# Attention in paired key tiles, and the conditioning's rows summed on VectorE with a short product on TensorE

## The chip, the cores and the metric

One core of a Trainium2 chip runs the whole kernel in one launch. The metric is the device time in microseconds (us). The engines that matter are TensorE (PE in the profile, PEld for its weight loads), VectorE (DVE), ScalarE (ACT), GpSimd (POOL) and SyncE (SP), whose queue issues most of the loads. Every engine works through its instructions in an order that is fixed when the kernel is built, and waits on semaphores for what others owe it.

## The reference, cut to what matters

The network is four layers on 256 rows (and, in the first layer, 256 rows of context) of width 1024, all in float32. The first two are "trunk" layers, the last two "hybrid" layers (a gated delta rule and a convolution branch). This is what the change touches:

```
def trunk_layer(x, ctx, c, c_ctx, p, ...):
    shift, scale, gate = split(silu(c) @ p['w_ada'] + p['b_ada'], 3)
    shift_c, scale_c, gate_c = split(silu(c_ctx) @ p['w_ada'] + p['b_ada'], 3)
    h  = x   * (1 + scale)   + shift          # context: hc, with the _c rows
    ... = split(h @ p['w_in'], pts)           # q, k, v, gates, decay inputs, ...
    y_attn = softmax(q k^T / 8) v * silu(a_g) # 8 heads of 64 on 2 key/value heads
    # gated linear attention (decay from (h @ w_a) @ a2 + ab), a spatial gating
    # unit, three branches merged, then
    x_new = layer_norm(ALPHA * x + gate * out, ...)
```

Layer 0 attends with 256 latent rows over 512 keys and with 256 context rows over 256 keys; layer 1 with the latent rows alone. `w_ada` is 1024 by 3072 for each layer: its product with the two vectors silu(c) and silu(c_ctx) gives shift, scale and gate, which this text calls the conditioning's rows. The hybrid layers need a small product of the same kind as the decay inputs (16 columns, called wab below).

## The kernel before

**Numbers.** A weight arrives as a 128x1024 piece of 512 KB through SP's queue into a ring of three buffers (`raw`, L232). `split` (L212) makes two fp32r halves of it, the high one by a cast on ScalarE (L214, `wh`) and the low one by a subtraction on VectorE (L215, `wl`). `mm3` (L220) multiplies with three fp32r matmuls: high by high, high by low, low by high. All of them go through one helper, so they carry the line L218; transposes carry L227.

**Order of the work.** A scheduler at build time sets one order per engine. It takes the program's order as priority, except where a piece is marked urgent, or is held `behind` another instruction. Layer 0 of the trunk starts with the conditioning of shift and scale for layer 0 (L417, in the first 43 us), then come the attention and the spatial gating unit together (about 49 to 252 us), the gated linear attention and the branches (to about 523 us) and the output norm. `PACES` (L170) says how many units of the branches are taken between the steps of the linear attention.

**The conditioning's rows.** What remains of them (gate of layer 0; shift, scale and gate of layer 1) is made by the generator `adaln` (L993) out of `ada_part` (L424). There are 4 parts of 8 pieces. For each piece the weight of 128x1024 is loaded into the same ring, and four plain f32 matmuls with a stationary of 128x32 (silu of the two vectors in its columns) and 256 moving columns each go side by side into four column tiles of the array (L433). Each f32 matmul has two records in the profile. The generator is drawn on between other steps of the layer (`fill`, L1004).

**Attention** (L628 to L770). For each tile of 128 rows and each pair of heads, the queries are transposed and split (`qh`, `ql`, 128x256, two buffers each), two score products per head follow (L218, `px<-kk,qh` and `px<-kk,ql`), then the maximum on VectorE (L748), the exponential on ScalarE (L749) and the norm on VectorE (L753). The probabilities are transposed for two key tiles at once into one bank (L227), split into `ph` (ScalarE) and `pl` (VectorE), and multiplied with the split values `vh` and `vl` by `mm3`: six matmuls of 256 columns for a tile, a key/value head and a key tile, taken over its two pairs. There are 24 such triples in layer 0 and 16 in layer 1, 40 in all.

**Small products.** The decay inputs (L773 to L797) and the wab product (start of `delta`, L1318) take `mm3` with a stationary of 32 and of 16 columns: three matmuls for each of 8 slices.

Of the kernel before, what the change touches and what calls it, by code (L numbers as in the profile page):

```python
# [17 lines left out]
P = 128  # L18
# [162 lines left out]
class Builder:  # L181
# [100 lines left out]

    def gemm_mv(self, keys, actT, tiles, evac):
# [31 lines left out]
    def build(self):  # L315
        nc, tc, io = self.nc, self.tc, self.io
        self.filler = iter(())
        with tc.tile_pool(name="const", bufs=1) as cp, \
# [23 lines left out]
            self.zero = cp.tile([P, 32], F32, name="zero")  # L342
            nc.vector.memset(self.zero, 0.0)
# [15 lines left out]
    def first_block(self):  # L359
        self.hTh = self.t(self.act, [P, KT, 512], F32R, tag="hTh")  # L360
        self.hTl = self.t(self.act, [P, KT, 512], F32R, tag="hTl")
        self.paT = self.t(self.act, [33, 512], tag="paT")
        self.nc.vector.memset(self.paT[32:33, :], 1.0)
# [7 lines left out]
    def start(self, sp):  # L371
# [30 lines left out]
        for name, to in (("mask", self.mask), ("maskc", self.maskc)):  # L402
            m = self.t(sp, list(to.shape), tag=name)
            nc.sync.dma_start(m, io[name])
            nc.gpsimd.tensor_copy(to, m)
# [18 lines left out]
    def ada_part(self, pool, l, part, out):  # L424

        nc = self.nc
        row = self.t(pool, [P, 256], tag="arow")
        nc.scalar.dma_start(row, self.io["bada"][l, part])
        ps = self.pa()
        for k in range(8):  # L430
            raw = self.raw(("ada", l, part, k))
            for q in range(4):
                self.nc.tensor.matmul(ps[32 * q:32 * q + 32, :256], self.sc[:, k, :], raw[:, 256 * q:256 * (q + 1)],  # L433
                                      start=k == 0, stop=k == 7, tile_position=(0, 32 * q))
            if k < 7:
                yield
        if part == 2:
            nc.vector.tensor_tensor(row, ps[:, :256], row, ALU.add)
            for v in ((0, 1) if l == 0 else (0,)):
                for q2 in range(2):  # L440
                    pt = self.psg()
                    for b in range(2):
                        r = 32 * (2 * q2 + b) + v
                        self.mm(pt[:, b * 256:(b + 1) * 256], self.ident[:, r:r + 1].to_broadcast([P, P]), row, True, True)

                    nc.scalar.activation(out[v][:, q2 * 512:(q2 + 1) * 512], pt, AF.Copy, scale=0.5)
        else:
            nc.vector.scalar_tensor_tensor(row, ps[:, :256], self.upper, row, ALU.add, ALU.add)
            pt = self.psg()
            for c in range(2):  # L450
                self.tr(pt[:, c * P:(c + 1) * P], row[:, c * P:(c + 1) * P])
            for a in range(2):
                src = pt[:, :256].rearrange("p (c a b v) -> p a b c v", c=2, a=2, b=2)[:, a, :, :, 0:2]
                dst = out[:, a, 4 * part:4 * part + 4, :].rearrange("p (b c) v -> p b c v", b=2)
                nc.vector.tensor_copy(dst, src)
        yield

    def trunk(self, l):
# [4 lines left out]
        with tc.tile_pool(name=f"m{l}", bufs=1) as mp:  # L463
            self.mp = mp
            if l == 0:
                self.yraw_a = self.big([P, 4, TN], tag="ya")
                self.yraw_g = self.big([P, 4, TN], tag="yg")
                self.m = [self.big([P, 4, TN], tag=f"m{i}") for i in range(2)]
# [6 lines left out]
            next(self.decay, None)  # L475
            with tc.tile_pool(name=f"sgu{l}", bufs=1) as sp:
                self.attention(l)
                self.sgu(l, sp)
            if l == 0:
                self.filler = self.adaln(mp)  # L480
            tgp = mp if l else tc.alloc_tile_pool(name="tg", bufs=1, side="right", reuse_waits="tile")
            units = self.units(l, tgp)
            pre0, rate0, mid, rate1 = PACES[l]
            for n, rate, hp in ((pre0, rate0, 0), (mid, rate1, 1)):
                for _ in range(int(n)):
                    next(units, None)
                due = 0.0
                for _ in self.gla(l, hp):
                    due += rate
                    while due >= 1:  # L490
                        due -= 1
                        next(units, None)
            for _ in units:
                pass
            self.fill(4)
            for _ in self.gate_y(l, G_G, self.yraw_g):
                pass
            with tc.tile_pool(name=f"late{l}", bufs=1, reuse_waits="tile") as lp:
# [5 lines left out]
                self.fill(32)  # L504
                if l:
                    self.out_ln(l)
                else:
                    tgp.release()
# [3 lines left out]
    def units(self, l, tgp):  # L512
# [4 lines left out]
        yield from self.gates(l, M_G, "tg", tgp)  # L517


    def sgu(self, l, sp):  # L520
# [36 lines left out]
        for g in range(4):  # L557
# [3 lines left out]
            mix = self.t(sp, [P, nt, P], tag="mix")  # L561
# [66 lines left out]
    def attention(self, l):  # L628
        nc, tc, io = self.nc, self.tc, self.io
        T0, TN = self.T0, self.TN  # L630
        with tc.tile_pool(name=f"att{l}", bufs=1, reuse_waits="tile") as ap:
# [59 lines left out]
            for i in range(4):  # L691
# [21 lines left out]
                vh[i] = self.t(ap, [P, 2, 64], F32R, tag=f"vh{i}")  # L713
                vl[i] = self.t(ap, [P, 2, 64], F32R, tag=f"vl{i}")
                self.split(vh[i], vl[i], kv[i][:, 128:256].rearrange("p (g d) -> p g d", g=2))
# [12 lines left out]
            for i in self.tiles:  # L728
                nk = 256 if i < 2 else 512
                for pr in range(4):  # L730
                    g = pr // 2
                    tp = self.ps()
                    if pr % 2 == 0:
                        du = self.t(ap, [P, 4, 2, 64], tag="du", bufs=2)
                        nc.scalar.copy(du, qkv[i][:, pr * P:(pr + 2) * P].rearrange("p (a b) -> p a b", a=4)[:, :, None, :].to_broadcast([P, 4, 2, 64]))
                    for a in range(2):
                        self.tr(tp[:, a * P:(a + 1) * P], du[:, pr % 2 * 2 + a].rearrange("p a b -> p (a b)"))
                    qh = self.t(ap, [P, 256], F32R, tag="qh", bufs=2)
                    ql = self.t(ap, [P, 256], F32R, tag="ql", bufs=2)
                    self.split(qh, ql, tp[:, :256])  # L740
                    mx = self.t(self.small, [P, 2], tag="mx")
                    sm = self.t(self.small, [P, 2], tag="sm")
                    pp = self.t(ap, [P, 2, nk], tag="pp", bufs=2)
                    for a in range(2):
                        s = self.ps()
# [1108 lines left out]
```

## Time and profile before

| | us |
|---|---|
| median of three runs | 1475.38 (1471.76 to 1478.45) |
| the profiled execution's own time | 1476.65 |
| its span | 1475.0 |
| TensorE busy in the span | 1406.7 (95%) |
| VectorE busy | 1024.1 (69%) |
| ScalarE busy | 846.9 (57%) |
| GpSimd busy | 70.2 (5%) |

All times below are of the profiled execution; its span leaves 1.65 us around it. The granted clock of TensorE was 0.99 of full speed over the span, so 2.4 GHz nearly throughout. "Busy" of TensorE is the union of matmul records, which overlap: from one start to the next is the better price of a matmul.

### The profile page before, as it was taken

How to read it: one execution, taken by the hardware profiler on the slowest of the kernel's cores; microseconds unless marked ns; L12 is line 12 of the kernel's file. 1: busy time of each engine (PE TensorE's matmuls, PEld its weight loads, DVE VectorE, ACT ScalarE, POOL GpSimd, SP SyncE). 2: the span in 40 equal slices, each digit the busy share in tenths (PEclk: the TensorE clock that was granted, in tenths of full speed). 3: DMA queues.
4: the chain of work that ended last, by engine and by line, in shares of the span. 5: the costliest groups of instructions: out<-in, count | busy, mean ns of one | idle time of the engine just before them, and what ended most of it. 6: DMA issues, size and time to landing. Idle time of an engine off the chain costs nothing.

```text
span 1475.0 us, 33026 instructions
## 1 busy us (share of the span) xinstructions
PE 1406.7 (95%) x13736; PEld 1233.2 (84%) x13736; DVE 1024.1 (69%) x2017; ACT 846.9 (57%) x1530; POOL 70.2 (5%) x228
## 2 busy tenths in 40 slices
PE   7999999999999999999999999879999999989998
PEld 4887778767876778998999999869889998979997
DVE  3576752874277248879847748877998776799885
ACT  2455644643374233555658576468695657967654
POOL 0000000110011000120000001011000000000000
PEclk9999999999999999999999999989999999999999
DMA  9321123234333346433324434614333553433362
GB/s 380 133 72 60 59 84 115 93 108 151 104 114 105 129 137 206 146 111 123 101 87 143 131 115 137 212 58 135 116 98 128 170 173 101 131 102 107 124 196 91
DMA packets 52901, 187.47 MB, mean 127 GB/s; under 512 B 6148, under 2 KB 7556, under 8 KB 52752
## 3 DMA queue, kind: packets, MB, share of 16 engines
q1 hardware_dynamic: 49248, 176.63, 36.3%
q0 software_dynamic: 2208, 7.35, 1.6%
q8 instruction: 108, 1.77, 0.5%
q10 hardware_dynamic: 1296, 1.39, 0.3%
q14 instruction: 41, 0.34, 0.1%
HBM read 184.29 MB, written 1.05 MB: 126 GB/s over the span
## 4 chain that ended last, share of the span: by engine, by line
PE 76%; DVE 10%; ACT 8%; issue 3%; DMA 2%; POOL 0%; SPq 0%; ACTq 0%; DVEq 0%; POOLq 0%
PE pg L218 57%; PE px L218 11%; PE px L227 3%; ACT wh L214 3%; DVE wl L215 2%; DMA raw<-in_W 2%; PE pa L433 1%; PE px L916 1%; DVE u L1721 1%; PE pa L218 1%; PE pa L417 1%; PE px L972 1%; PE px L1534 1%; PE px L950 1%; DMA araw<-in_W 0%
## 5 line engine op out<-in xcount | busy, mean ns | idle before, releaser
L215 DVE TENSOR_TENSOR wl<-raw,wh 128x1024 fp32r<-128x1024 f32 (+1 forms) x278 | 338.6, 1220 | 217.9 <-ACT wh L214 216.5
L218 PE MATMUL pg<-hTh,wh 128*128 128x256 f32 (+1 forms) x1440 | 460.2, 320 | 0.8 <-DVE mix L562 0.8
L214 ACT CAST wh<-raw 128x1024 fp32r<-128x1024 f32 (+1 forms) x278 | 289.3, 1043 | 284.0 <-PE pg L218 198.2
L218 PE MATMUL pg<-hTh,wl 128*128 128x256 f32 (+1 forms) x1440 | 450.1, 313 | 0.0
L218 PE MATMUL pg<-hTl,wh 128*128 128x256 f32 (+1 forms) x1440 | 449.9, 312 | 0.0
L218 PEld LDWEIGHTS pg<-hTh,wh 128*128 128x128 f32 x1440 | 271.5, 189 | 30.4 <-issue 12.5
L218 PEld LDWEIGHTS pg<-hTl,wh 128*128 128x128 f32 x1440 | 271.9, 189 | 15.9 <-issue 3.0
L218 PEld LDWEIGHTS pg<-hTh,wl 128*128 128x128 f32 x1440 | 271.1, 188 | 14.8 <-issue 0.4
L1721 DVE SCALAR_TENSOR_TENSOR u<-cpad,cols,u 128x256 f32<-128x256 f32 x240 | 104.6, 479 | 0.9
L218 PE MATMUL pg<-big,wh 128*128 128x512 f32 (+1 forms) x384 | 100.9, 345 | 4.2 <-DVE tg L620 1.4
L218 PE MATMUL pg<-wh,hTh 128*128 128x256 f32 x320 | 91.4, 286 | 0.6 <-ACT kd L817 0.6
L218 PE MATMUL pg<-wl,hTh 128*128 128x256 f32 x320 | 91.1, 285 | 0.0
L218 PE MATMUL pg<-wh,hTl 128*128 128x256 f32 x320 | 91.0, 285 | 0.0
L218 PEld LDWEIGHTS pg<-big,wh 128*128 128x128 f32 x384 | 65.9, 188 | 15.5 <-DVE big L215 2.1
L218 PE MATMUL pg<-wh,mh 128*128 128x256 f32 x272 | 77.1, 285 | 0.3 <-DVE y L1281 0.3
L218 PE MATMUL pg<-wl,mh 128*128 128x256 f32 x272 | 76.8, 283 | 0.3 <-DVE wl L215 0.3
L218 PE MATMUL pg<-wh,ml 128*128 128x256 f32 x272 | 76.8, 283 | 0.0
L218 PE MATMUL pg<-big,wl 128*128 128x512 f32 (+1 forms) x192 | 65.2, 341 | 0.0
L218 PEld LDWEIGHTS pg<-wh,hTh 128*128 128x128 f32 x320 | 61.2, 191 | 1.2 <-ACT kd L817 1.1
L218 PEld LDWEIGHTS pg<-wh,hTl 128*128 128x128 f32 x320 | 61.2, 191 | 0.1
L218 PEld LDWEIGHTS pg<-wl,hTh 128*128 128x128 f32 x320 | 61.1, 191 | 0.0
L218 PEld LDWEIGHTS pg<-wh,mh 128*128 128x128 f32 x272 | 51.9, 191 | 0.8 <-issue 0.4
(457 smaller groups left out, 2526.5 us busy)
## 6 DMA issues: line engine op xcount, KB each, us to landing
raw<-in_W SPq DMA_DIRECT2D x314, 512.0 KB, 3.5
araw<-in_W SPq DMA_DIRECT2D x16, 512.0 KB, 9.5
xT<-in_xT SPq DMA_DIRECT2D x4, 512.0 KB, 9.9
yg<-in_xtok POOLq DMA_DIRECT2D x2, 512.0 KB, 4.3
m<-in_xtok POOLq DMA_DIRECT2D x2, 512.0 KB, 6.1
nwrow<-in_nwrow POOLq DMA_DIRECT2D x2, 512.0 KB, 4.3
arow<-in_bada ACTq DMA_DIRECT2D x4, 128.0 KB, 2.8
wsT<-in_sguw POOLq DMA_DIRECT2D x2, 256.0 KB, 4.0
```

The source lines that it names most:

```text
L214: self.nc.scalar.copy(h, src)
L215: self.nc.vector.tensor_tensor(l, src, h.bitcast(F32), ALU.subtract)
L218: self.last_mm = self.nc.tensor.matmul(out, lhsT, rhs, start=start, stop=stop).ins
L227: self.nc.tensor.transpose(out, in_, self.ident[:k, :k])
L417: nc.tensor.matmul(ps[32 * g:32 * g + 32, :P], self.sc[:, k, :], raw[:, o:o + P], start=k == 0, stop=k == 7, tile_position=(0, 32 * g))
L433: self.nc.tensor.matmul(ps[32 * q:32 * q + 32, :256], self.sc[:, k, :], raw[:, 256 * q:256 * (q + 1)], start=k == 0, stop=k == 7, tile_pos ...
L916: nc.tensor.matmul(out[o, a, :], x[:, a, o], y[:, a, o], start=True, stop=True, tile_position=(0, 32 * b))
L950: nc.tensor.matmul(pa[ks, a, ts], e[ch, li, a, ks], qe[ch, li, a, ts], start=True, stop=True, tile_position=(64 * d, s0))
L972: nc.tensor.matmul(o[r], blk[r, h, :], v[r, i, h * P:(h + 1) * P], start=False, stop=True, tile_position=(32 * b, 32 * b))
L1534: nc.tensor.matmul(pu[quad(b), o:o + 32], src[quad(b), dr, h, :], rhs[quad(b), dr, h, :], start=True, stop=True, tile_position=(32 * b, 32 ...
L1721: nc.vector.scalar_tensor_tensor(out, src, w, out, ALU.mult, ALU.add)
```

## The change

Three places change. First, the remaining conditioning's rows: VectorE multiplies each 128x1024 piece with a per-partition scalar and adds it to a running sum (56 instructions: one for each piece and vector, three parts with two vectors and one with one), and 28 matmuls of 256 columns then add the sums over the 128 partitions, with a stationary that picks a row (`ada_row`). The pieces are loaded through GpSimd's queue into two buffers of their own. The sums are emitted behind attention and gating unit in the program, but may start from the beginning of the attention. Second, attention works on a tile and a key/value head (four query heads, two pairs) at a time: `qh` and `ql` are 128x512 in one buffer each, the transposed probabilities of both pairs for one key tile go into one bank, are copied once (one key tile on ScalarE, the next on VectorE) and are multiplied in plain f32 with the unsplit values, the two pairs in two column tiles of 64. Third, the decay and wab products hold the high and low half side by side in one stationary, so two matmuls do instead of three; the sum of the halves falls to the small product that follows.

```diff
-            self.split(*self.wab, wab)            # wab and decay alike
+    def mm_stack(self, out, w, k, h, l, start, stop):
+        w = w[:, k * 64:(k + 1) * 64]
+        self.mm(out[0:64], w, h, start, False)
+        self.mm(out[0:64], w, l, False, stop)
...
-    def ada_part(self, pool, l, part, out):
+    def ada_sums(self, raws, acc, l, part):
+        vs = (0,) if (l, part) == (1, 2) else (0, 1)
+        for k in range(8):
+            raw = self.t(raws, [P, 1024], tag="adaw")
+            nc.gpsimd.dma_start(raw, self.io["W"][INDEX["ada", l, part, k]])
+            for v in vs:
+                sc = self.sc[:, k, v:v + 1]
+                if k == 0:
+                    nc.vector.tensor_scalar(acc[:, v], raw, sc, None, ALU.mult)
+                else:
+                    nc.vector.scalar_tensor_tensor(acc[:, v], raw, sc, acc[:, v], ALU.mult, ALU.add)
...
+    def ada_row(self, pool, sums, l, part, tag):
...
-        for k in range(8):
-            raw = self.raw(("ada", l, part, k))
-            for q in range(4):
-                self.nc.tensor.matmul(ps[32 * q:32 * q + 32, :256], self.sc[:, k, :], raw[:, 256 * q:256 * (q + 1)],
-                                      start=k == 0, stop=k == 7, tile_position=(0, 32 * q))
+        for v, acc in enumerate(sums):
+            for q in range(4):
+                nc.tensor.matmul(ps[32 * q:32 * q + 32, :256], self.pick[:, 2 - v:34 - v], acc[:, 256 * q:256 * (q + 1)],
+                                 start=v == 0, stop=v == len(sums) - 1, tile_position=(0, 32 * q))
...
+            raws = None if l else tc.alloc_tile_pool(name="ada", bufs=2, reuse_waits="tile")
+            ada = iter(()) if l else self.adaln(mp, raws)
             with tc.tile_pool(name=f"sgu{l}", bufs=1) as sp:
                 self.attention(l)
                 self.sgu(l, sp)
+            next(ada, None)
+            next(ada, None)
...
-                for pr in range(4):
-                    g = pr // 2
+                for g in range(2):
...
-                    qh = self.t(ap, [P, 256], F32R, tag="qh", bufs=2)
-                    ql = self.t(ap, [P, 256], F32R, tag="ql", bufs=2)
-                    self.split(qh, ql, tp[:, :256])
+                    qh = self.t(ap, [P, 512], F32R, tag="qh")
+                    ql = self.t(ap, [P, 512], F32R, tag="ql")
+                    self.split(qh, ql, tp)
...
-                        ph = self.t(ap, [P, 512], F32R, tag="ph")
-                        pl = self.t(ap, [P, 512], F32R, tag="pl")
-                        self.split(ph, pl, tq)
-                        for b in range(2):
-                            kt = 2 * k2 + b
-                            self.mm3(pv, vh[kt][:, g], vl[kt][:, g], ph[:, b * 256:(b + 1) * 256], pl[:, b * 256:(b + 1) * 256],
-                                     kt == 0, kt == nkt - 1)
+                            pT = self.t(ap, [P, 512], tag=f"pT{b}")
+                            (nc.vector.tensor_copy if b else nc.scalar.copy)(pT, tq)
+                            pTs.append(pT)
+                        for b in range(2):
+                            kt = 2 * k2 + b
+                            for j in range(2):
+                                nc.tensor.matmul(pv[64 * j:64 * j + 64, :256], kv[kt][:, 128 + 64 * g:192 + 64 * g], pTs[b][:, j * 256:(j + 1) * 256],
+                                                 start=kt == 0, stop=kt == nkt - 1, tile_position=(0, 64 * j))
...
+    def adaln(self, pool, raws):
+        parts = ((1, 0, "m0"), (1, 1, "m1"), (0, 2, "yg"), (1, 2, None))
+        for l, part, tag in parts:
+            acc = self.big([P, 2, 1024], tag=tag) if tag else self.t(raws, [P, 1, 1024], tag="acc", bufs=1)
+            with self.behind(self.pool_start):
+                sums.append(self.ada_sums(raws, acc, l, part))
+        yield
+        with self.behind(self.last_mm):
+            for n in range(2):
+                self.ada_cols(*self.ada_row(raws, sums[n], *parts[n][:2], "adaw"), n, self.mod1)
...
-        self.split(wah, wal, raw)
+        self.stack(wa, raw)
...
-            self.mm3(pa[0:32, :n], wa[0][:, k * 32:(k + 1) * 32], wa[1][:, k * 32:(k + 1) * 32],
-                     self.hTh[:, k, a:a + n], self.hTl[:, k, a:a + n], k == 0, k == KT - 1)
+            self.mm_stack(pa[:, :n], wa, k, self.hTh[:, k, a:a + n], self.hTl[:, k, a:a + n], k == 0, k == KT - 1)
```

VectorE's order at the start of layer 0's attention, before (`ss` are the sums for the norms of queries and keys, `nw` the steps of their square root, L215 the low halves of weights and values):

```order
L215 TENSOR_TENSOR wl_1555<-raw_1552,wh_1554 128x1024
L215 TENSOR_TENSOR vl_97_693<-qkv_60_491,vh_96_692 128x128
L215 TENSOR_TENSOR vl_100_706<-qkv_61_492,vh_99_705 128x128
L215 TENSOR_TENSOR vl_103_719<-qkv_62_493,vh_102_718 128x128
L686 TENSOR_REDUCE ss_644<-sq_645 128x10
L686 TENSOR_REDUCE ss_644<-sq_648 128x10
L686 TENSOR_REDUCE ss_644<-sq_651 128x10
L215 TENSOR_TENSOR wl_1561<-raw_1558,wh_1560 128x1024
L215 TENSOR_TENSOR wl_1671<-raw_1668,wh_1670 128x1024
```

and there now:

```order
L448 TENSOR_SCALAR m_377_1944<-adaw_1945,sc 128x1024 x2
L450 SCALAR_TENSOR_TENSOR m_377_1944<-adaw_1949,sc,m_377_1944 128x1024
L215 TENSOR_TENSOR wl_1355<-raw_1352,wh_1354 128x1024
L450 SCALAR_TENSOR_TENSOR m_377_1944<-adaw_1949,sc,m_377_1944 128x1024
L450 SCALAR_TENSOR_TENSOR m_377_1944<-adaw_1953,sc,m_377_1944 128x1024
L727 TENSOR_REDUCE ss_636<-sq_637 128x10
L450 SCALAR_TENSOR_TENSOR m_377_1944<-adaw_1953,sc,m_377_1944 128x1024
L727 TENSOR_REDUCE ss_636<-sq_640 128x10
L450 SCALAR_TENSOR_TENSOR m_377_1944<-adaw_1957,sc,m_377_1944 128x1024 x2
L727 TENSOR_REDUCE ss_636<-sq_643 128x10
```

The values' low halves are gone, and the sums of the first pieces stand between the steps of the norms. All 56 sums stand from here to the end of the gating unit, ahead of the first instruction of the linear attention's decays.

VectorE's order within one step of the attention in layer 0, before (one pair of heads: low half of the queries, two maxima, the norm):

```order
L215 TENSOR_TENSOR ql_928<-px_922,qh_927 128x256
L748 TENSOR_REDUCE mx_931<-px_934 128x1
L748 TENSOR_REDUCE mx_931<-px_939 128x1
L751 RECIPROCAL rc_944<-sm_932 128x2
L753 TENSOR_SCALAR pp_933<-pp_933,rc_944 128x256 x2
L215 TENSOR_TENSOR pl_954<-px_948,ph_953 128x512
```

and now (a key/value head with its two pairs; `th` and `big` belong to the gating unit):

```order
L450 SCALAR_TENSOR_TENSOR m_386_1977<-adaw_1998,sc,m_386_1977 128x1024
L215 TENSOR_TENSOR ql_942<-px_934,qh_941 128x512
L605 TENSOR_TENSOR big_1625<-big_1625,th_1789 128x512
L788 TENSOR_REDUCE mx_945<-px_948 128x1
L788 TENSOR_REDUCE mx_945<-px_953 128x1
L788 TENSOR_REDUCE mx_962<-px_965 128x1
L788 TENSOR_REDUCE mx_962<-px_970 128x1
L791 RECIPROCAL rc_958<-sm_946 128x2
L450 SCALAR_TENSOR_TENSOR m_386_1977<-adaw_1998,sc,m_386_1977 128x1024
L793 TENSOR_SCALAR pp_173_947<-pp_173_947,rc_958 128x256 x2
L791 RECIPROCAL rc_975<-sm_963 128x2
L450 SCALAR_TENSOR_TENSOR m_386_1977<-adaw_2002,sc,m_386_1977 128x1024
```

Sums now stand between the maximum and the norm of one step.

GpSimd's queue before, from the loads of the gating unit's weights on (`wsT`, `bs`; `a` is the small matrix of the decays, `S` the state of the linear attention):

```order
L525 DMA wsT_1547<-in_sguw 128x512
L527 DMA bs_1549<-in_sgub 128x512
L806 DMA a_465_2377<-in_a 33x256
L888 MEMSET S_2610 64x256 x2
```

and the end of the same stretch now, where `adaw` are the pieces of the conditioning's weights:

```order
L444 DMA adaw_2053<-in_W 128x1024
L444 DMA adaw_2056<-in_W 128x1024
L444 DMA adaw_2059<-in_W 128x1024
L852 DMA a_452_2322<-in_a 65x256
L934 MEMSET S_2549 64x256 x2
L444 DMA adaw_2062<-in_W 128x1024
L444 DMA adaw_2065<-in_W 128x1024
```

Thirty loads of such pieces, each waiting for the sums two pieces earlier, stand between `bs` and `a`, and two behind `S`.

## Rows read from the trace of the kernel before

**Rows 1.** The page: engines (busy us, share of span, instructions), then the chain's shares
```profile
PE 1406.7 (95%) x13736; PEld 1233.2 (84%) x13736; DVE 1024.1 (69%) x2017; ACT 846.9 (57%) x1530; POOL 70.2 (5%) x228
PE 76%; DVE 10%; ACT 8%; issue 3%; DMA 2%; POOL 0%; SPq 0%; ACTq 0%; DVEq 0%; POOLq 0%
```

**Rows 2.** Windows: length; busy us (instructions) of PE, PEld, DVE, ACT, POOL; clock; DMA
```profile
49.00:252.00 203.00, 200.32 (x1212) 164.17 (x1211) 124.07 (x249) 104.15 (x230) 2.23 (x5) 1.00 0.26 85
260.00:320.00 60.00, 58.66 (x806) 42.08 (x805) 46.94 (x99) 34.85 (x59) 8.69 (x41) 1.00 0.28 92
320.00:420.00 100.00, 99.68 (x612) 76.81 (x611) 42.27 (x72) 44.16 (x65) 0.61 (x2) 1.00 0.43 138
420.00:523.00 103.00, 101.95 (x1065) 73.96 (x1067) 53.67 (x108) 41.34 (x67) 8.20 (x40) 1.00 0.32 105
1030.00:1106.00 76.00, 70.75 (x1629) 65.17 (x1629) 72.02 (x151) 59.50 (x122) 0.78 (x12) 0.98 0.34 107
1290.00:1327.00 37.00, 33.17 (x994) 29.44 (x995) 35.32 (x80) 24.67 (x45) 0.65 (x10) 0.95 0.33 104
```

**Rows 3.** Source line L433, whole run, then its part in 49 to 252 us
```profile
L433 PE MATMUL pa<-raw,sc x256: 378/380/405, 133.2 to 523.3; 128*32 128x256 f32 x128
...
L433 PE MATMUL pa<-raw,sc x40: 378/391/404, 133.2 to 245.8; 128*32 128x256 f32 x40
```

**Rows 4.** Timeline of TensorE around one piece: start us, length us, engine, line
```profile
264.72 0.40 PE L218 MATMUL pg<-big,wl 128*128 128x512 f32 x1
265.05 0.64 PE L433 MATMUL pa<-raw,sc 128*32 128x256 f32 x8
265.62 0.50 PE L218 MATMUL pg<-hTh,wh 128*128 128x512 f32 x1
265.96 0.39 PE L218 MATMUL pg<-hTl,wh 128*128 128x512 f32 x1
266.19 0.39 PE L218 MATMUL pg<-hTh,wl 128*128 128x512 f32 x1
```

**Rows 5.** Timeline of TensorE, products with the values in layer 0
```profile
98.98 0.27 PE L218 MATMUL px<-ph,vl 128*64 128x256 f32 x1
99.09 0.28 PE L218 MATMUL px<-ph,vh 128*64 128x256 f32 x1
99.21 0.28 PE L218 MATMUL px<-pl,vh 128*64 128x256 f32 x1
99.33 0.28 PE L218 MATMUL px<-ph,vl 128*64 128x256 f32 x1
```

**Rows 6.** Groups by shape, whole run: count, busy us, mean ns, idle before
```profile
L218 PE MATMUL px<-ph,vh 128*64 128x256 f32 x80 | 23.9, 299 | 0.3
L218 PE MATMUL pg<-hTh,wabh 128*16 128x256 f32 x16 | 5.8, 361 | 0.2 <-ACT hTh L1219 0.2
L1721 DVE SCALAR_TENSOR_TENSOR u<-cpad,cols,u 128x256 f32<-128x256 f32 x240 | 104.6, 479 | 0.9
L753 DVE TENSOR_SCALAR pp<-pp,rc 128x512 f32<-128x512 f32 x32 | 14.5, 484 | 0.5
```

**Rows 7.** Groups by shape on VectorE, 49 to 252 us
```profile
L215 DVE TENSOR_TENSOR wl<-raw,wh 128x1024 fp32r<-128x1024 f32 x26 | 31.8, 1223 | 35.1 <-ACT wh L214 34.7
L215 DVE TENSOR_TENSOR pl<-px,ph 128x512 fp32r<-128x512 f32 x24 | 16.5, 689 | 13.6 <-ACT ph L214 13.4
L215 DVE TENSOR_TENSOR ql<-px,qh 128x256 fp32r<-128x256 f32 x16 | 6.7, 418 | 3.6 <-ACT qh L214 3.5
```

**Rows 8.** DMA issues: count, KB each, us from issue to landing
```profile
raw<-in_W SPq DMA_DIRECT2D x314, 512.0 KB, 3.5
...
xT<-in_xT SPq DMA_DIRECT2D x4, 512.0 KB, 9.9
yg<-in_xtok POOLq DMA_DIRECT2D x2, 512.0 KB, 4.3
m<-in_xtok POOLq DMA_DIRECT2D x2, 512.0 KB, 6.1
```

## What the change was predicted to do

> **What bounds the kernel now.** I read the page first: TensorE is busy for 95% of the span and holds 76% of the chain, VectorE 69% and 10% [rows 1]. So a matmul taken away is worth its time almost everywhere, and work given to VectorE is free only where VectorE has room. Which room it has is read by stage, from the windows [rows 2]. From 49 to 252 us, layer 0's attention with the gating unit, TensorE is busy for 200.3 of 203.0 us and VectorE for 124.1: 79 us of room. From 260 to 523 us TensorE is as full (58.7 of 60, 99.7 of 100, 102.0 of 103), with VectorE at 54%. Two later windows are the measure for a full VectorE: at 72.0 of 76 us busy (95%) it leaves TensorE idle for 5.3 us (7%), and at 35.3 of 37 (95%) for 3.8 us (10%, at a clock of 0.95), against 1.3% in the first window. The order says that all 56 sums fall into that first window. The case is decided by the matmul time saved and by whether 79 us of room suffice for it without holding up the chain score, maximum, exponential, norm, transposition, product.
>
> **The conditioning's products on TensorE.** The line has 256 records, two for each of 128 matmuls: 32 pieces of 8 records [rows 3]. The price of a piece is what it displaces. A product of 512 columns steps by 0.23 us (265.96 to 266.19). Around the piece, 264.72 would be followed by a start at 264.95 and comes to its next product only at 265.62, which is 0.67 us late, and the step after it is 0.34 instead of 0.23, another 0.11: 0.78 us together [rows 4]. 32 x 0.78 = 25.0 us go. What comes is 28 matmuls of the same width in four column tiles, 7 such groups, 5.5 us. Net 19.5 us, of which the 5 groups (40 records) that stood inside 49 to 252 us are 3.9 and the 27 behind it 21.1 [rows 3]; the 5.5 us that come fall into the first window.
>
> **Products with the values.** Six matmuls of 256 columns for a tile, head group and key tile: 80 records of each of three alike kinds, 240 in all, 40 sixes [rows 6]. They step by 0.12 us (98.98, 99.09, 99.21, 99.33), so a six costs 0.71 us [rows 5]. Now there are two f32 matmuls in two column tiles, four records. No such pair is in the trace; the nearest row is the conditioning's group, eight records of the same width in four column tiles for 0.67 + 0.11 us. If two tiles cost as much as four, 0.78, nothing is gained (40 x -0.07 = -3 us). If the records run side by side at the fp32r step, 2 x 0.12 = 0.24, it gains 40 x 0.47 = 19 us. I take half of the group's 0.57 us from its start to the next one's, and its whole after-effect, 0.29 + 0.11 = 0.40, since half of the records stand there: 40 x 0.31 = 12.4 us, 7.4 for the 24 in layer 0 and 5.0 for the 16 in layer 1. The row shows the 0.11 us after a group. The Trainium skill, TensorEngine Tiling (Array Packing), Key Properties, says that a change of the tiling mode drains TensorE and that different tiles load and multiply in parallel. The trace agrees with both, and by the first the short pairs, which stand between untiled products, would pay a drain at each end and come nearer to the upper bound than to the lower.
>
> **The stacked products.** One of three matmuls goes, 8 slices each. A wab product has 16 matmuls per kind over two layers [rows 6], at the 256-column step 16 x 0.12 = 1.9 us; layer 1's decay inputs, in two halves of 256, as much. Layer 0's lie in the first 43 us, where loads set the pace; I count them at nothing (1.9 us if they decide). Sum 3.8 us, between 0 and 5.7.
>
> **VectorE.** A sum is a SCALAR_TENSOR_TENSOR of 128x1024. The trace has that form at 256 columns, 479 ns [rows 6]; a plain two-operand operation takes 418 ns at 256 and 1223 at 1024 [rows 7]. So 1.22 us, or 1.22 + 0.06 with the difference at 256; I take 1.25 for 49 of them. The seven first products are TENSOR_SCALAR, 484 ns at 512 columns [rows 6], so 0.97 at most, say 0.9. 61.3 + 6.3 = 67.6 us come. In layer 0 the 24 `pl` (16.5 us) and 16 `ql` (6.7) go [rows 7], and 12 copies of 512 columns and 8 `ql` of 512 at 0.69 us come (13.8): -9.4. VectorE's need between 49 and 252 us becomes 124.1 + 67.6 - 9.4 = 182.3 us. TensorE's is 203.0 - 3.9 - 7.4 + 5.5 = 197.2, with its old 2.7 us of idle time. VectorE would be 92% busy. That is just below the two full windows, where TensorE lost 7 and 10%; here it lost 1.3% with VectorE at 61%. Between these I put the extra loss at 3%, 6 us. Bounds: nothing, and 15 us at 9%.
>
> **The loads of the pieces.** They leave SP's weight ring (32 of 314 loads; cover, not path) and go through GpSimd's queue into two buffers, so a load starts when the sums two pieces earlier are done. Adding the durations of VectorE's ordered rows between those sums and the first sum on the new piece gives about 3.6 to 3.8 us for pieces 2, 3, 4, 6 and 7, 2.6 to 4.7 for the last five, and mostly 6 to 16 between. A load of this size through that queue took 4.3 us, and 6.1 in the other case [rows 8]. At 4.3 us the shortfalls sum to some 7 us, at 6.1 to 25, but a late piece lengthens the time of the next but one, so I halve them: 3.5 to 12.5. A VectorE that waits holds the weights' low halves behind it and so TensorE's next products, but waits that it would have had anyway are in the count. I take 4. Of the queue itself: the small matrix of the decays now lands behind thirty pieces, near the end of the window and still before its use at about 260 us. I count that at nothing; late by a piece it is 4.3 us.
>
> **The sum.** -19.5 - 12.4 - 3.8 = -35.7 on TensorE. Back: 6 and 4 us in the first window; and 4 us of the 21.1 that go behind it, since the pieces there were also filler in gaps of the linear attention, which lost TensorE only 1.3 of 60 us [rows 2] and will show more of its waits. ScalarE has half the casts less and as much room as before. Total -21.7 us: the profiled 1476.65 becomes 1455.0, and since that run is 1.27 us above the median of 1475.38, the median 1453.7. I say 1453.
>
> **Rivals.**
> *All of it on the path.* VectorE's room suffices, and the pairs run side by side: -35.7 to -42 (with 19 in place of 12.4), so 1433 to 1440. For it: VectorE's need is still under TensorE's, and the scheduler can run products of the gating unit under the chain. Against: two full windows that both cost TensorE.
> *VectorE becomes the bound of layer 0's attention.* Single-buffered `qh` and `ql`, four maxima and four exponentials in one step, and sums of 1.25 us between maximum and norm. If 15 us are lost by fullness, 10 by loads and 4 more in the gaps of the linear attention behind it, -35.7 + 29 = -7: 1464 to 1475. For it: sums stand in the order right inside the chain. Against: the order has the gating unit's products for TensorE meanwhile.
> *Late pieces stop VectorE (slower).* Loads through the queue land late, and the fixed order makes VectorE wait at each. Loads of this size took 9.9 us at the start of the kernel [rows 8]. At that landing the shortfalls of the pieces sum to some 94 us, halved 47: -35.7 + 4 + 6 + 47 = +21, 1497. It decides from a landing of about 8 us, where the halved shortfalls reach 30 us and the gain is gone. Against: the queues were nearly idle there, 0.26 busy [rows 2], and 4.3 and 6.1 us are what that queue did. What could delay it is VectorE itself; the norm's TENSOR_SCALAR at 484 ns for 512 columns against 689 for a two-operand one [rows 6, 7] is faster by the column. The Trainium skill, SBUF — State Buffer, Who interferes with whom and the "DVE blocks DMA" trap before it, says that a DMA from GpSimd's queue has its descriptors written by GpSimd, and starves while VectorE runs a copy or a scalar operation in a mode that takes the port pair they share. The trace has no load beside such work often enough to show it.
> *The column tiles bring nothing.* At 0.78 us for a pair the products lose 3 us in place of gaining 12.4: 1469.
>
> **Chances.** The forecast (1443 to 1462) 0.50; all of it on the path 0.17; VectorE the bound 0.16; late pieces 0.10; tiles that bring nothing 0.07. Half a percent, 7.4 us, is about what a measurement of this kernel tells from no change. Faster by more than that (below 1468) are the first two, a third of the third and half of the last, 0.76; within it 0.14; slower, the late pieces, 0.10. The range for 8 in 10 runs from 1435, inside the best case, to 1475, the end of the case of the bound VectorE.
>
> **What would show it.** In the changed profile: no 256 records but 56 for the conditioning; a sum of 1.22 to 1.28 us; TensorE with 36 us less to do; the linear attention's start near 49 + 197 + 10 = 256 us where it was at 252, with VectorE near 88% before it (182 of 207); and everything behind that start 26 us shorter (21.1 + 5.0 + 3.8 - 4). Idle time of VectorE that ends with a piece's landing, over 15 us of it, would show the late pieces. Wrong is the forecast if the first stretch loses more than 20 us against its 197, or if TensorE's idle time grows behind it by as much as was taken out.

## The result, and the profile after

The changed kernel takes 1457.9 us (1456.51 to 1461.37, four runs) where the kernel before takes 1476.1: a ratio of 0.9883 with a 95% interval of 0.9865 to 0.9901, 18 us less by the medians. The forecast was 1453, in a range of 1435 to 1475. The profiled execution took 1456.51 us, its span is 1454.8. The page's engine line and the shares of the chain, to be set beside [rows 1]:

```profile
PE 1375.5 (95%) x13420; PEld 1210.5 (83%) x13420; DVE 1061.0 (73%) x2033; ACT 831.6 (57%) x1490; POOL 88.8 (6%) x260
PE 66%; DVE 12%; ACT 11%; issue 5%; DMA 5%; POOL 0%; SPq 0%; DVEq 0%; ACTq 0%; POOLq 0%
```

TensorE lost 31 us of busy time and 10 points of the chain; ScalarE and DMA took three of them each, VectorE and issue two each. To see where the 20 us of span came from, the kernel is cut at the same three instructions in every version: the first Abs of the linear attention's decays in layer 0 (`ab`), the first output row of layer 0 (`h`) and the first row of the hybrid layers (`xs`). Their groups before, then after (behind the durations stand the first and the last start):

```profile
L840 ACT ACTIVATE ab<-px x8: 592/597/597, 254.4 to 864.4; 128x512 f32<-128x512 f32 x8
L1147 ACT ACTIVATE h<-px,B,G x28: 439/466/543, 607.8 to 630.0; 128x128 f32<-128x128 f32 x28
L1194 DVE TENSOR_TENSOR xs<-x,nwrow x18: 419/426/689, 959.7 to 1469.0; 128x256 f32<-128x256 f32 x16, 128x512 f32<-128x512 f32 x2
```

```profile
L886 ACT ACTIVATE ab<-px x8: 592/598/602, 264.5 to 849.2; 128x512 f32<-128x512 f32 x8
L1201 ACT ACTIVATE h<-px,B,G x28: 439/462/536, 595.0 to 617.9; 128x128 f32<-128x128 f32 x28
L1248 DVE TENSOR_TENSOR xs<-x,nwrow x18: 419/425/682, 945.4 to 1448.5; 128x256 f32<-128x256 f32 x16, 128x512 f32<-128x512 f32 x2
```

The first window (from the last scaling of the input, `xT`, at 44.7 and 45.3 us, to `ab`) grew from 209.7 to 219.2 us; `ab` to `h` fell from 353.4 to 330.5; `h` to `xs` from 351.9 to 350.4; the rest from 515.3 to 509.4. The rest varies by itself: over the kernels below whose hybrid layers are the same it is 507.8 to 515.2. So the gain is the 22.9 us between the linear attention's start and the first output row, and the first window gave 9.5 back. Windows of before and then of after over the first stretch (length, busy us of PE, PEld, DVE, ACT, POOL, the granted clock, DMA):

```profile
44.70:254.40 209.70, 207.02 (x1247) 168.23 (x1245) 127.30 (x258) 109.26 (x239) 2.94 (x6) 1.00 0.26 84
```

```profile
45.30:264.50 219.20, 206.77 (x1209) 163.73 (x1208) 178.76 (x298) 102.38 (x216) 19.22 (x37) 0.98 0.44 147
60.00:75.00 15.00, 12.23 (x94) 12.03 (x93) 14.11 (x14) 6.06 (x10) 1.58 (x3) 0.92 0.62 195
120.00:135.00 15.00, 11.85 (x80) 8.25 (x78) 12.94 (x29) 8.60 (x24) 0.53 (x1) 1.00 0.27 94
135.00:150.00 15.00, 12.15 (x64) 9.75 (x63) 12.47 (x29) 6.64 (x23) 0.44 (x1) 0.89 0.08 29
```

TensorE is busy as long as before (206.8 against 207.0 us) and idle for 12.4 in place of 2.7 us, 8.8 of them in the last three rows. The granted clock, 1.00 before, is 0.92 and 0.89 in two of these rows: TensorE ran for part of them at the lower of its two levels, 1.2 GHz, behind a pause of 2.8 us that ended at 72.1 and one of 2.2 us that ended at 137.4. An estimate from the two rows, (0.08 + 0.11) x 15 us, says that up to 2.9 us of the window went that way, inside the busy time. The sums of the first two parts and all the pieces' loads read thus:

```profile
L450 DVE SCALAR_TENSOR_TENSOR m<-adaw,sc,m x28: 1266/1279/1287, 57.9 to 158.2; 128x1024 f32<-128x1024 f32 x28
L448 DVE TENSOR_SCALAR m<-adaw,sc x4: 727/747/753, 54.8 to 103.1; 128x1024 f32<-128x1024 f32 x4
adaw<-in_W POOLq DMA_DIRECT2D x32, 512.0 KB, 3.8
```

At 60 to 87 us VectorE shows what the sums displace. The norm of queries and keys is a chain of small steps of 0.2 us; before, its twelve steps ran from 69.2 to 71.7 us with nothing between them. Timeline of VectorE, the first and the last step before, then after:

```profile
69.19 0.19 DVE L689 TENSOR_SCALAR ss<-ss 128x40 f32<-128x40 f32 x1
...
71.51 0.20 DVE L265 SCALAR_TENSOR_TENSOR rs<-nw_b,nw_y 128x40 f32<-128x40 f32 x1
```

```profile
75.05 0.18 DVE L730 TENSOR_SCALAR ss<-ss 128x40 f32<-128x40 f32 x1
75.14 1.28 DVE L450 SCALAR_TENSOR_TENSOR m<-adaw,sc,m 128x1024 f32<-128x1024 f32 x1
76.34 0.18 DVE L252 TENSOR_SCALAR nw_i<-ss 128x40 int32<-128x40 int32 x1
...
79.63 1.28 DVE L450 SCALAR_TENSOR_TENSOR m<-adaw,sc,m 128x1024 f32<-128x1024 f32 x1 [0.79 <-DMA adaw<-in_W]
80.83 0.20 DVE L265 SCALAR_TENSOR_TENSOR nw_y<-nw_b,nw_y 128x40 f32<-128x40 f32 x1
80.94 1.28 DVE L450 SCALAR_TENSOR_TENSOR m<-adaw,sc,m 128x1024 f32<-128x1024 f32 x1
...
87.02 0.20 DVE L265 SCALAR_TENSOR_TENSOR rs<-nw_b,nw_y 128x40 f32<-128x40 f32 x1
```

The chain takes 12 us in place of 2.5 and starts 6 us later, and the first output of attention in layer 0 comes at 124.5 instead of 100.0. The products with the values, on TensorE (layer 1, after):

```profile
706.64 0.40 PE L218 MATMUL pg<-big,wh 128*128 128x256 f32 x2
707.11 0.65 PE L812 MATMUL px<-pT,qkv 128*64 128x256 f32 x4
707.70 0.87 PE L227 MATMUL px<-ident,pp 128*128 128x128 f32 x6
```

A pair takes 0.59 us to the next start, and two fp32r steps of 0.12 before it would have led to 706.88, so the entry costs up to 0.2 more. The six before cost 0.71 by their steps [rows 5], but they paid for an entry too (layer 0, before):

```profile
97.60 0.40 PE L218 MATMUL pg<-hTh,wh 128*128 128x512 f32 x1
97.98 0.33 PE L218 MATMUL px<-ph,vh 128*64 128x256 f32 x1
98.15 0.40 PE L218 MATMUL pg<-hTl,wh 128*128 128x512 f32 x1
```

The product with the values starts 0.38 us behind one that is elsewhere followed after 0.23, and holds TensorE for 0.17 in place of 0.12. Added up from start to start over both timelines, idle time left out and the delays before them counted, the 24 sixes of layer 0 took 20.1 us and the 24 pairs 16.4, the 16 of layer 1 13.1 and 11.0: about 0.83 us for a six and 0.68 for a pair. That is an estimate of 5.9 us saved on TensorE.

### The profile page after: what moved, and what is told of

Read it like the earlier page. It is cut to its first block, busy times and chain, and to the rows that moved or that the text cites. A ratio compares the mean times of both kernels' runs of the same rounds, so it can differ in the third digit from the quotient of the medians.

```text
span 1454.8 us, 32364 instructions
## 1 busy us (share of the span) xinstructions
PE 1375.5 (95%) x13420; PEld 1210.5 (83%) x13420; DVE 1061.0 (73%) x2033; ACT 831.6 (57%) x1490; POOL 88.8 (6%) x260
## 4 chain that ended last, share of the span: by engine, by line
PE 66%; DVE 12%; ACT 11%; issue 5%; DMA 5%; POOL 0%; SPq 0%; DVEq 0%; ACTq 0%; POOLq 0%
PE pg L218 51%; PE px L218 7%; DVE wl L215 3%; ACT wh L214 3%; PE px L227 3%; DMA raw<-in_W 2%; DVE u L1776 2%; DMA adaw<-in_W 1%; PE px L812 1%; PE px L962 1%; PE pa L431 1%; PE px L1018 1%; PE px L996 1%; ACT L1503 1%; DVE hTl L215 1%
## 5 line engine op out<-in xcount | busy, mean ns | idle before, releaser
L215 DVE TENSOR_TENSOR wl<-raw,wh 128x1024 fp32r<-128x1024 f32 x276 | 336.9, 1224 | 192.7 <-ACT wh L214 173.6
L218 PE MATMUL pg<-hTh,wh 128*128 128x256 f32 (+1 forms) x1440 | 455.2, 317 | 1.6 <-issue 1.6
L218 PE MATMUL pg<-hTh,wl 128*128 128x256 f32 (+1 forms) x1424 | 444.0, 312 | 0.7 <-DVE wl L215 0.7
```

Of the source, the lines that this page charges most:

```text
L215: self.nc.vector.tensor_tensor(l, src, h.bitcast(F32), ALU.subtract)
L218: self.last_mm = self.nc.tensor.matmul(out, lhsT, rhs, start=start, stop=stop).ins
```

## The experiments

All are compared with the kernel before by ratio, since it took 1475.3 to 1476.9 us in the sessions of these runs; "window" is from the last scaling of the input to `ab`.

**One part undone or done alone.** The old attention with the rest kept:

```diff
-                for g in range(2):          # the whole of attention() as changed
+                for pr in range(4):         # ... as before
...
```

> The changed kernel with the old attention (pairs of heads, split probabilities, six fp32r matmuls for a key tile), the sums and the stacked products kept. In the changed trace four records of a product with the values start 0.58 us before the next one (121.53 to 122.11), where 0.40 was forecast and a six cost 0.71. Theory (the products with the values were mis-sized and gain only 40 x 0.13 = 5 us less what they pay after them): 1458 to 1465 us. Rival (they gain the 12 us forecast and the loss is elsewhere): 1469 to 1473.

1472.2 us, ratio 0.9976 (0.9963 to 0.9990). The rival's number. But its reason, 12 us of matmul time, does not show in the next run: the old rows with the new attention,

```diff
...
-            ada = iter(()) if l else self.adaln(mp, raws)
+                self.filler = self.adaln(mp)        # ada_part() as before
```

> The changed kernel with the old conditioning's rows (32 pieces through the weight ring, 128 matmuls), the new attention and the stacked products kept. Theory (the rows are worth 19.5 us on TensorE less some 10 us of a full VectorE, so nearly half of the whole gain; the rest gives 5 + 4): 1466 to 1471. Rival (attention carries most of the gain, the sums cost as much as they save): 1458 to 1462.

1475.52 us, ratio 0.9994 (0.9982 to 1.0006): neither expectation. And the stacked products alone:

```diff
-            self.mm3(pa[0:32, :n], wa[0]..., wa[1]..., ...)
+            self.mm_stack(pa[:, :n], wa, k, ...)
```

> The kernel before with only the decay and wab products stacked (two matmuls for three). Theory: 32 matmuls of 0.12 us go from the path, 3.8 us: 1472. Rival (they lie where TensorE waits for loads or for VectorE anyway): 1476, no change.

1475.86 us, ratio 0.9996 (0.9986 to 1.0005): no change that can be told. So the attention is worth 0.3 us without the sums (1475.86 to 1475.52) and 14 us with them (1472.2 to 1457.9); the sums are worth some 4 us without the new attention (1475.86 to 1472.2, where the two intervals just touch). The traces show part of the reason. The scaling of attention's outputs in layer 0, first to last, before, with the new attention, with the sums, and with both (the last three with the stacked products):

```profile
L770 ACT ACTIVATE ya<-px x32: 255/268/272, 100.0 to 214.4; 64x128 f32<-64x128 f32 x32
```

```profile
L787 ACT ACTIVATE ya<-px x32: 268/272/276, 101.4 to 182.9; 64x128 f32<-64x128 f32 x32
```

```profile
L811 ACT ACTIVATE ya<-px x32: 255/269/272, 117.7 to 254.4; 64x128 f32<-64x128 f32 x32
```

```profile
L817 ACT ACTIVATE ya<-px x32: 268/272/276, 124.5 to 232.6; 64x128 f32<-64x128 f32 x32
```

Half as many steps end 32 us earlier, which alone bought nothing: TensorE had other products until the window's end at 255.5 us. The sums start the attention 18 to 25 us later and stretch it, from 114.4 to 136.7 us with the old steps; with these it outlasts most of the other products. Windows of the version with sums and old attention:

```profile
215.00:225.00 10.00, 9.94 (x63) 8.44 (x62) 8.76 (x13) 4.47 (x10) 1.70 (x3) 1.00 0.71 225
225.00:235.00 10.00, 7.78 (x57) 4.96 (x55) 7.44 (x18) 4.99 (x14) 0.00 (x0) 1.00 0.10 33
245.00:255.00 10.00, 6.25 (x34) 4.04 (x33) 3.72 (x7) 6.62 (x16) 0.61 (x2) 0.92 0.01 2
```

From 226 us the weight stream is over (DMA 0.10 to 0.01) and TensorE waits for steps of the softmax chain: 2.2 and 3.8 us in the last two rows. The whole windows with the stacked products alone, with the new attention and the old rows, and with the sums and the old attention:

```profile
44.80:256.60 211.80, 207.28 (x1239) 168.50 (x1238) 127.33 (x258) 109.28 (x239) 2.95 (x6) 0.99 0.26 83
44.00:255.50 211.50, 204.31 (x1191) 160.35 (x1190) 117.37 (x234) 101.56 (x215) 2.95 (x6) 0.98 0.26 83
45.30:272.80 227.50, 213.47 (x1257) 173.30 (x1256) 188.42 (x322) 110.10 (x240) 19.46 (x37) 0.98 0.44 141
```

Without the sums the new attention takes 3.0 us of busy time from TensorE and adds 2.7 us of idle time (7.2 for 4.5), so the window stays. With the sums it takes 6.7 us of busy time (213.5 to 206.8) and 1.6 of idle time (14.0 to 12.4). Layer 1 takes 351.2 us against 350.7 without the sums, and 350.4 against 354.2 with them, there nearly all of it idle time (13.6 against 17.2). Why the new attention counts only beside the sums is not parted further. Behind the window the sums give the same with either attention: `ab` to `h` is 330.6 and 330.5 us, and 352.9 and 352.7 with the old rows.

**A repeat.** The hold on two parts' sums

```diff
-            with self.behind(self.pool_start):
+            with self.behind(self.pool_start if len(sums) < 2 else self.last_mm):
```

> The changed kernel with the sums of the last two parts (24 of 56) held until the gating unit's last product, so that they stand beside the linear attention, where VectorE has room. Theory (the first window is long because VectorE is full): the linear attention's first decay, at 264.5 us now, comes 6 to 9 us earlier, and the time is 1449 to 1454. Rival (the chain of the new attention step is what is long, not VectorE's load, or the sums hold up the linear attention as much): 1457 to 1462.

left the order of every engine as it was, since it holds only instructions of TensorE's own queue. 1461.5 us, ratio 0.9901 (0.9885 to 0.9917), window 222.1: that is the changed kernel once more, so it decides between neither expectation, and says how far a repeat may lie off, 3 us in a window.

**VectorE's load.** Forty-two adding sums left out:

```diff
-                else:
+                elif k == 7:
```

> The changed kernel with 42 of the 49 adding sums left out (only the first and the last piece of a part are taken; the rows are then not the reference's); all loads and all else stay. It takes about 54 us from VectorE. Theory (a full VectorE lengthens the first window): the linear attention's first decay, at 264.5 us, moves to 252 to 256 and the time to 1446 to 1450. Rival (the loads, or the new step's chain): it stays above 261 and the time above 1455.

1468.07 us, ratio 0.9949 (0.9930 to 0.9968), window 231.6: the rival's side, and 10 us slower than the changed kernel, which neither expected. The last piece's sum now stood in VectorE's order early, behind seven loads. Waits from 45 to 150 us (engine, tile and line, what ended the wait; us in all, times, longest):

```profile
DVE m L450 <- DMA adaw<-in_W: 12.3, 2, 7.6
ACT du L760 <- DVE qkv L742: 8.3, 2, 7.8
PE px L227 <- ACT du L760: 12.2, 2, 7.9
```

A late piece on VectorE stops the queries' copy and then TensorE. It shows that mechanism, but says nothing on load. Sums of half the width do:

```diff
-nc.vector.scalar_tensor_tensor(acc[:, v], raw, sc, acc[:, v], ALU.mult, ALU.add)
+nc.vector.scalar_tensor_tensor(acc[:, v, 0:512], raw[:, 0:512], sc, acc[:, v, 0:512], ALU.mult, ALU.add)
```

> The changed kernel with every adding sum on 512 of the 1024 columns (the second half of the rows keeps the first piece's product alone; the rows are not the reference's). Loads, their number and the count of instructions stay; a sum of 1.28 us becomes some 0.73, so about 27 us leave VectorE in the first window. Theory (VectorE's load lengthens that window): from the last input row to the linear attention's decays 219.2 us become 208 to 213, the time 1447 to 1452. Rival (the landing of the pieces or the step's own chain lengthens it, and a shorter sum only waits longer): above 216 and 1455 to 1460.

1458.05 us, ratio 0.9893 (0.9876 to 0.9910), as the rival said:

```profile
45.00:264.00 219.00, 206.38 (x1210) 162.04 (x1208) 154.10 (x298) 101.18 (x217) 19.40 (x37) 0.98 0.45 147
```

VectorE has 25 us less to do and the window is the same. The run says a second thing. Its chain of norms and its attention outputs in layer 0:

```profile
76.26 0.18 DVE L731 TENSOR_SCALAR ss<-ss 128x40 f32<-128x40 f32 x1
...
80.27 0.20 DVE L265 SCALAR_TENSOR_TENSOR rs<-nw_b,nw_y 128x40 f32<-128x40 f32 x1
```

```profile
L818 ACT ACTIVATE ya<-px x32: 268/272/274, 114.3 to 211.9; 64x128 f32<-64x128 f32 x32
```

The chain takes 4.2 us where it took 12, the outputs start 10 us and end 21 us earlier than in the changed kernel, and the window is no shorter. So neither the chain's delay nor the end of the attention can be shown to set the changed kernel's window; the engines' orders differ in several hundred lines too. Nor does it help to move 24 sums out of it:

```diff
...
+        hold = self.gla_dve          # VectorE's last step of the decays
+        for p in parts[2:]:
+            add(*p, hold)
```

> The changed kernel with the sums of the last two parts (24 of 56, some 30 us of VectorE) behind VectorE's last step of the linear attention's decays, so after the first window. Theory (the first window is VectorE's, and behind it VectorE has room): the window shrinks from 219.2 to 206 to 212 us, the linear attention and branches behind it stay at 330 to 334, the time is 1447 to 1452. Rival (the sums delay the linear attention's chain, which has VectorE at 78% in its first 60 us): that part grows by 6 us or more, 1455 to 1460.

1459.88 us, ratio 0.9906 (0.9888 to 0.9924): window 217.2, `ab` to `h` 334.5: 2.0 us gained in the one, which is within a repeat, and 4.0 lost in the other. The time is the rival's, the growth short of its 6 us.

**The pieces' landings.** Three buffers, SP's queue, and both:

```diff
-            raws = None if l else tc.alloc_tile_pool(name="ada", bufs=2, ...)
+            raws = None if l else tc.alloc_tile_pool(name="ada", bufs=3, ...)
...
-            nc.gpsimd.dma_start(raw, ...)
+            nc.sync.dma_start(raw, ...)
```

> The changed kernel with three buffers for the pieces in place of two. VectorE's 8.1 us of idle time before sums that ended with a piece's landing should go. Theory (late pieces cost part of what is lost in the first window): 1453 to 1456, idle time before sums under 2 us. Rival (VectorE would have waited for something else): 1457 to 1459.

> The changed kernel with the pieces' loads on SP's queue in place of GpSimd's. If a load through GpSimd's queue were held up by VectorE, its landing, 3.8 us in the median, would fall to the weights' 3.5 and the waits of 8.1 us would shrink: 1454 to 1457. Rival: SP's queue is in order too, and a piece that waits for its buffer holds the weights behind it: TensorE waits for weights in the first window and the time is 1465 or more.

> The changed kernel with the pieces' loads on SP's queue and three buffers for them. Each alone gave 1452 and 1454 against 1457.9 and 1461.5 of the changed order. Theory (both take away the same wait for a piece's landing): together no better than the one, 1450 to 1454. Rival (two different waits): 1445 to 1449.

1454.27 us (0.9862, 0.9838 to 0.9886), 1451.95 us (0.9838, 0.9819 to 0.9858) and 1455.96 us (0.9874, 0.9857 to 0.9891); windows 213.6, 213.7 and 216.3. Each alone takes some 5 us from the window, both together no more. A landing is 3.8 us through GpSimd's queue and 3.7 through SP's, so it is not the queue's speed. Nor do VectorE's waits for a piece follow the window: 8.1 us in the changed kernel, 3.7 with three buffers (under 2 were expected), 3.2 with both, but 8.8 with SP's queue alone:

```profile
DVE acc L450 <- DMA adaw<-in_W: 7.8, 5, 2.2
DVE m L450 <- DMA adaw<-in_W: 1.0, 2, 0.8
```

The order of VectorE and TensorE differs in several hundred lines too, and what takes the 5 us stays open. The lowest of all is the version with SP's queue. Its interval is just clear of the changed kernel's, but not so with a third buffer added, so no more than a likely gain is shown. With the late gate sums on top

> Pieces' loads on SP's queue, three buffers, and the sums of the last two parts behind the linear attention's decays. Theory (VectorE's load and the landings are two costs of the first window): window 203 to 208 us, 1441 to 1447, the best of all. Rival (one of them hides the other): 1448 to 1453.

it is 1458.54 us, ratio 0.9882 (0.9863 to 0.9902), window 214.8, `ab` to `h` 333.0: neither number.

**The column tiles.** One plain f32 product of 512 columns for two of 256 side by side:

```diff
-                                nc.tensor.matmul(pv[64 * j:64 * j + 64, :256], ..., tile_position=(0, 64 * j))
+                            self.mm(pv[0:64], kv[kt][...], pTs[b], kt == 0, kt == nkt - 1)
```

> The changed kernel with one plain f32 matmul of 512 columns for both pairs in place of two of 256 columns in two column tiles. The changed trace shows a plain f32 product of 512 columns as two records in about 0.95 us, and the tiled pair in 0.58. Theory (the price of the pair is that of one f32 product of 256 columns, two passes, and the two tiles do run side by side): 40 x 0.37 = 15 us more, 1470 to 1474. Rival (the tiles run one after the other and the pair pays for all four passes): 1456 to 1460.

1468.48 us, ratio 0.9948 (0.9931 to 0.9965), 10.6 us more than tiled: less than the theory's 15 and clear of its rival. Two of its products in a row:

```profile
705.41 1.93 PE L218 MATMUL px<-pT,qkv 128*64 128x512 f32 x4
707.27 1.09 PE L227 MATMUL px<-ident,pp 128*128 128x128 f32 x8
```

1.86 us for two, 0.93 for one, against 0.59 for a tiled pair. The tiles do run side by side. What the pair pays is a plain f32 product's pace: 0.93 us for two records of 512 columns is 0.23 for a record of 256, twice the fp32r step of 0.12.

## Why the prediction was right, point by point

- **The conditioning's products** (19.5 us, of which 21.1 behind the first window, less 4 for gaps they had filled): the direction and nearly the size. Behind the window 22.9 us went, 21.4 of them TensorE's busy time (349.1 to 327.7) and 1.5 its idle time, so the gaps did not show and the 4 us were not due.
- **The products with the values** (12.4 us) are the term that was mis-sized: about 6 us on TensorE by the timelines, 0.15 for each in place of 0.31. The step that failed took half of a group of four tiles' 0.57 us [rows 4] for two tiles, 0.40 with the after-effect. Tiles run side by side, so two take as long as four, 0.59, and 0.68 with the entry. The other end of the range, "as much as four", was nearer; that the pair still gains comes from the six, which cost 0.83 with an entry of its own that the forecast's 0.71 left out. In the time the gain does not show without the sums: 1475.52 against 1475.86, because TensorE idles 2.7 us more. The forecast survived, since the sum had room.
- **The stacked products** (3.8 us): 1.0 us by the medians, not told from nothing.
- **VectorE and the loads** (6 + 4 us in the first window): TensorE's idle time there grew by 9.7 us, so the size was right. Neither reason is shown. VectorE's busy share, 82% of the window, is not it: with 25 us less of it the window stayed at 219.0. The landings are not shown either: the window shrinks by some 5 us with a third buffer or with another queue, but with the other queue VectorE waits for pieces as long as before (8.8 us against 8.1). A size that comes out right while its reasons do not is luck as far as these runs show. The Trainium skill, SBUF — State Buffer, Who interferes with whom, says that GpSimd, which writes the descriptors of its own DMAs, is blocked while VectorE runs a copy, a cast or a `tensor_scalar` in a mode that takes both ports. The median landings of 3.8 us through GpSimd's queue and 3.7 through SP's show no such delay.
- **What was not in the sum.** One is the clock: an estimate of up to 2.9 us of the first window at the lower level, behind pauses of TensorE. The other is the attention's run through layer 0, which is itself a length: with the sums and the old steps it starts 18 us later, takes 22 us longer and ends where TensorE has little else. The new attention's shorter run and smaller products give 8.3 us of that window back (227.5 to 219.2), 6.7 of busy and 1.6 of idle time; how the two share them is not shown.
- **The sum**: -21.7 us forecast, -20.2 in the profiled spans. By stage, against the forecast: first window 5.3 worse (9.5 for 4.2: half of the values' 7.4 of layer 0 missing, and the clock), linear attention and branches 5.8 better (-22.9 for -17.1), layer 1 5.4 worse (-1.5 for -6.9: the values gave 2.1 of 5.0 on TensorE), hybrid layers 4.0 better, inside their spread. Misses of opposite sign made the total look better than its terms; that it came within 1.5 us is luck.
- **The signs named beforehand**: a sum takes 1.28 us, as said; TensorE has 31 us less to do for 36; the linear attention starts at 264.5 for 256; what follows is 30 us shorter for 26; VectorE's waits for pieces, 8.1 us, stay under the 15 that would have shown late pieces.

Open is what holds TensorE in the first window of the changed kernel. Part of it needs no sums: the new attention alone has 7.2 us of idle time where the stacked products alone have 4.5. For the rest neither VectorE's load, nor the chain of norms, nor the waits for pieces explains the runs. Sums held until the norms are done were not tried.

## What to carry to other kernels

Price a product by the pace of its own data type and by one tile's time, since tiles in parallel do not get cheaper by being fewer, and count the entry on both sides of the comparison. When work moves to an engine with room on average, look at which short chain it is dealt between: here 1.28 us sums between 0.2 us steps made 12 us of 2.5. But test whether that delay counts before it is called the cause: with shorter sums the chain took 4.2 us and the window was the same. And a part that buys nothing alone may be what makes another change pay, so undo the parts one at a time and together.

## What the runs showed of the hardware

A TENSOR_SCALAR of 128x1024 f32 took 0.75 us (0.9 was assumed), a SCALAR_TENSOR_TENSOR 1.28. An f32 product of 256 columns in four column tiles, in two, or in one holds TensorE for 0.57, 0.59 and (by halves of 0.93) about 0.47 us, so two or four tiles side by side took little longer than one.
